# Two macaron layers with a three-group token mixer: first transposes of the FFN one product later, and copies, table switch and gate product of the mixer reordered

## The chip, the cores and the metric

The kernel runs on one core of a Trainium2 chip. The metric is the time of one execution on the device in microseconds (us). TensorE is called PE, its weight loads PEld, VectorE DVE, ScalarE ACT, GpSimd POOL and SyncE SP. DVE, ACT, POOL and SP each work through their own list of instructions in order.

## The reference

Two layers (L = 2) work on one sequence of 256 tokens of 1024 numbers, all in float32. Each layer is a half-step SwiGLU FFN, a token mixer and a second half-step FFN, each followed by a residual and a layer norm:

```
for l in range(2):
    x = layer_norm(a*x + 0.5*swiglu(x, wg[l,0], wu[l,0], wd[l,0]), ...)
    x = layer_norm(a*x + token_mix(x, ...), ...)
    x = layer_norm(a*x + 0.5*swiglu(x, wg[l,1], wu[l,1], wd[l,1]), ...)
swiglu(x) = (silu(x @ wg) * (x @ wu)) @ wd        # 1024 -> 2816 -> 1024
```

`token_mix` projects the stream once into the columns of three groups. Group A is a sparse attention with three branches: over compressed tokens (blocks of 32 tokens through a small GELU network), over selected blocks and over a window, merged by sigmoid gates. Group B subtracts the token from trailing means over 2, 4, 8 and 16 positions and multiplies by small matrices. Group C is a gated linear attention in chunks of 64 tokens: its output is normalised per head (root mean square over 64), and multiplied by a weight and by `silu(r)`. The three outputs side by side go through one output projection.

## The kernel before, in words

**Precision.** A float32 weight tile is cut into a high part (`wh`, a copy by ACT that rounds) and a low part (`wl`, what DVE has left after subtracting the high part). Every product is three matmuls of one pass each: high by high, high by low, low by high. These cuts (splits) of the weights are most of what ACT and DVE do. There are four buffers each for `wh` and `wl` (2 x 1024 columns) and four for the raw weights (`raw`); SP issues the loads in order, as buffers come free.

**The FFN.** The 2816 columns are 11 chunks of 256 gate and 256 up columns; the 256 tokens are two tiles t = 0, 1 of 128. Chunks 0 and 1 are computed first, plainly (`glu`), into the accumulator banks `acc` of each tile. The middle of the FFN is written out by hand in `PLAN`, and there PE's order is pinned to the program's. `S2`, `S4`, `S6` and `S8` open a block of two chunks c and c+1 by two tiles, done by a fast scheme with seven products instead of eight. A product is 12 matmuls of 512 columns and is named by a digit. The weights of some products are sums of weight blocks, which DVE forms in a tile `fa` (`b["s"]`):

- product 1 uses chunk c, first half (`fd`); product 5 the sum of `fd` and `fb` (L147), after which POOL has the DMA add a further block into `fb` for product 7;
- product 6 (`f6`) adds `fc` to the sum and splits it by `split_both` in two halves: two copies on ACT (L241) and two subtractions on DVE (L242);
- product 3 splits `fc` and product 7 `fb`, both in one wide subtraction (L234); product 2 loads two `raw` tiles and splits them (L172, L173);
- product 4 (`f4`) adds those two `raw` tiles to the sum (L180) and splits it again by `split_both`.

Other letters of `PLAN`: `a10` and `b10` are the first and second half of chunk 10 for both tiles (plain products; weight splits at L261 and L263); `T0`, `T2`, ... transpose the gated products of two chunks (`h_T`, L541) and split them into `hi` and `lo`; `d0`, `d1`, ... multiply them by the down weights (`down`), into two `acc` banks for each tile that ACT has seeded with the residual (L304). The list of weight units is filled from the same `PLAN`, so loads and splits follow its order.

PSUM has eight banks: for each tile one `g`, one `tr` and two `acc`. In the middle, `g` and `tr` form a list of free banks (`self.free`), from which blocks, T and a10 take theirs.

Gate products are made by `gate` (ACT L446, DVE L447 into `hh`) for plain chunks and by `gated` (L529, L530) for the blocks.

**The mixer.** Its order is the list `ORDER`, but here nothing is pinned on PE: a planner orders each engine's instructions by program order, by its own assumed durations, and by marks: `high_priority` lets an instruction go ahead of others that are ready, `issue_after(x)` (in the kernel also `after(x)`) places it behind x on the same engine. The steps that matter here:

- `chunk_gates`: PE transposes `c3`, DVE copies the result to `gaT` (L650), PE multiplies it by a small weight (L652).
- `compress`: a chain of small DVE operations on 30 numbers per partition computes the GELU: reciprocal, product (L722), then a copy that repeats the result four times into `grep` (L723), which PE uses as weights (L726).
- `attention`: for tile 1, eight items; each has scores on PE, an exponential on ACT (L853), a normalisation on DVE (L857), transposes on PE into the tile's one `tr` bank (L331) and a copy of them by ACT into `pT` (L900).
- the entry `s` of `ORDER` loads ACT's table with Silu (L1085), behind the last exponential (`m.last_exp`).
- `gla_out`: PE computes `ob`, ACT squares it (L954), DVE sums (L956, L957), POOL takes the power -1/2 (L958), DVE multiplies `ob` by it (L959) and then by `grs`, which holds weight and gate (L961), and PE transposes the product (L331).

Of the kernel before, what the change touches and what calls it, by code (L numbers as in the profile page):

```python
# [10 lines left out]
def _warn_once_fixed(msg, *args, **kwargs):  # L11
# [7 lines left out]
F32 = mybir.dt.float32  # L19
# [3 lines left out]
AF = mybir.ActivationFunctionType  # L23
# [14 lines left out]

PLAN = ("S2 1 T0 5 a10 6 3 b10 7 2 d0 4 S4 1 T2 5 d1 6 3 d2 7 2 4 S6 d3 1 T4 5 6 d4 3 7 2 4 "
        "S8 d5 1 T6 5 6 d6 3 T10 7 2 4 d7 T8").split()

LAST = (10, 8, 9)
# [12 lines left out]
def build(ctx, tc, d):  # L57
# [76 lines left out]
    def seven(l, f, c):  # L134


        b = {}

        def load(to, c, q, pool, name, tag):
            b[to] = pool.tile([128, 2048], F32, name=name, tag=tag, bufs=1)  # L140
            for h, a in enumerate(gate_up(l, f, c, q)):
                last_dma[0] = nc.sync.dma_start(out=b[to][:, h * 1024:(h + 1) * 1024], in_=a)

        def add(x, y=None):
            for h in range(2):
                s = slice(h * 1024, (h + 1) * 1024)
                DVE.tensor_add(out=b["s"][:, s], in0=(b["s"] if y is None else y)[:, s], in1=x[:, s])  # L147

        def f1():
            load("11", c, 0, act, "fd", "lnp")  # L150
            return split_wide(b["11"])

        def f5():
            load("12", c + 1, 0, cst, "fb", "s_w1")
            b["s"] = cst.tile([128, 2048], F32, name="fa", tag="ks")
            add(b["12"], b["11"])
            for h, a in enumerate(gate_up(l, f, c + 1, 1)):
                nc.gpsimd.dma_start(out=b["12"][:, h * 1024:(h + 1) * 1024], in_=a, accum_op=ALU.add)  # L158
            return split_both(b["s"])

        def f6():
            load("22", c + 1, 1, mix, "fc", "pT")
            add(b["22"])
            return split_both(b["s"])

        def f2():
            b["21"] = []
            u = split_tiles()
            for a, (wh, wl) in zip(gate_up(l, f, c, 1), u):
                raw = wp.tile([128, 1024], F32, name="raw", bufs=4)  # L170
                last_dma[0] = nc.sync.dma_start(out=raw, in_=a)
                ACT.activation(out=wh, in_=raw, func=AF.Copy)  # L172
                DVE.tensor_sub(out=wl, in0=raw, in1=wh.bitcast(F32))  # L173
                b["21"].append(raw)
            return u

        def f4():
            for h, raw in enumerate(b["21"]):
                s = slice(h * 1024, (h + 1) * 1024)
                DVE.tensor_add(out=b["s"][:, s], in0=b["s"][:, s], in1=raw)  # L180
            return split_both(b["s"])

        return {"1": f1, "5": f5, "6": f6, "7": lambda: split_wide(b["12"]), "3": lambda: split_wide(b["22"]),
                "4": f4, "2": f2}

# [48 lines left out]
        DVE.tensor_sub(out=wl, in0=raw, in1=wh.bitcast(F32))  # L234
        return in_halves(u)

    def split_both(raw):
        u = split_tiles()
        for h, (wh, wl) in enumerate(u):
            s = slice(h * 1024, (h + 1) * 1024)  # L240
            ACT.activation(out=wh, in_=raw[:, s], func=AF.Copy)  # L241
            DVE.tensor_sub(out=wl, in0=raw[:, s], in1=wh.bitcast(F32))  # L242
        return u

    def after(ins):
        return tc.issue_after(ins.ins) if ins else ExitStack()
# [41 lines left out]
    def pe(ins):  # L288

        if pinned[0]:  # L290
            tc.keep_in_program_order(ins)
        last_pe[0] = ins
# [114 lines left out]
    class Ffn:  # L407
# [126 lines left out]
        def h_T(self, t, g):  # L534
            src = self.hh.pop((t, g))
            if 2 * g == NCH - 1:
                src = src[:1]
            n = 2 * len(src)
            which, p = self.bank()
            for i, x in enumerate(x[:, j * 128:(j + 1) * 128] for x in src for j in range(2)):  # L540
                pe(PE.transpose(p[:, i * 128:(i + 1) * 128], x, ident))  # L541
            with tc.high_priority():
                hi = mix.tile([128, 4, 128], F32R, name="hi", tag="P", bufs=4)
                lo = mix.tile([128, 4, 128], F32R, name="lo", tag="b2", bufs=4)
                split(hi[:, 0:n], lo[:, 0:n], p[:, 0:128 * n].rearrange("p (a b) -> p a b", a=n))
            self.h[t, g] = (hi, lo)
            self.free.append(which)

        def down(self, t, c):
            accs = self.accs[t]  # L550
# [77 lines left out]
    def chunk_gates(m, t):  # L628
# [18 lines left out]

        p = transposes(t, [c3])
        gaT = mt(t, "gaT", [128, 128])
        DVE.tensor_copy(out=gaT, in_=p[:, 0:128])  # L650
        zp = bank("tr", t)
        PE.matmul(zp[:, 0:128], sm["wa2"], gaT, start=True, stop=True)  # L652
        az = mt(t, "az", [128, 128])
# [48 lines left out]
    def compress(m):  # L702
# [16 lines left out]
        ACT.activation(out=gs, in_=gs, func=AF.Exp, scale=-2.0 * GELU_C)  # L719
        DVE.tensor_scalar(out=gs, in0=gs, scalar1=1.0, scalar2=None, op0=ALU.add)  # L720
        DVE.reciprocal(out=gs, in_=gs)
        DVE.tensor_mul(out=gs, in0=gs, in1=xg)  # L722
        DVE.tensor_copy(out=grep[:, :, :, 0:15], in_=gs[:, None, :, :].to_broadcast([128, 4, 2, 15]))  # L723
        kp = bank("tr", 1)
        gflat = grep.rearrange("p a b c -> p (a b c)")
        PE.matmul(kp[:, 0:128], sm["w2k"], gflat, start=True, stop=True)  # L726
# [94 lines left out]
    def attention(m, t):  # L821

        v = m.t[t]
# [68 lines left out]
        def transpose_p(i):  # L892
            pj = P.pop(i).rearrange("p a b -> p (a b)")
            p = transposes(t, [pj[:, k * 128:(k + 1) * 128] for k in range(4)])
            j, gs = items[i]
            if j == 0:

                pool, tag = (wp, "fb") if t == 0 or gs[0] else (mix, "pT")
                PT[gs[0]] = pool.tile([128, 4, 4, 128], F32, name=f"pT{t}", tag=tag, bufs=1)
            ACT.activation(out=PT[gs[0]][:, :, j, :], in_=p.rearrange("p (a b) -> p a b", a=4), func=AF.Copy)  # L900

        def values():

# [33 lines left out]
    def gla_out(m, t):  # L937
# [18 lines left out]
        DVE.tensor_reduce(out=ms[:, 0:4], in_=sq, axis=AX.X, op=ALU.add)  # L956
        DVE.tensor_scalar(out=ms[:, 0:4], in0=ms[:, 0:4], scalar1=1.0 / 64, scalar2=RMS_EPS, op0=ALU.mult, op1=ALU.add)  # L957
        POOL.tensor_tensor(out=ms[:, 4:8], in0=ms[:, 0:4], in1=mhalf, op=ALU.pow)  # L958
        DVE.tensor_tensor(out=sq, in0=ob4, in1=ms[:, 4:8, None].to_broadcast([128, 4, 64]), op=ALU.mult)  # L959
        sqf = sq.rearrange("p a b -> p (a b)")  # L960
        DVE.tensor_mul(out=sqf, in0=sqf, in1=v["grs"])  # L961
        p = transposes(t, [sqf[:, 0:128], sqf[:, 128:256]])
        split(cth[:, 6:8, :], ctl[:, 6:8, :], p[:, 0:256].rearrange("p (a b) -> p a b", a=2))

# [109 lines left out]
    for l in range(L):  # L1074
        ffn(l, 0, sums, None)
        m = m0[0] if l == 0 else Mix(l)
        att = [attention(m, t) for t in range(2)]
        out = [wout(m, t) for t in range(2)]
        for op in ORDER.split():
            t = int(op[1]) if len(op) > 1 else 0  # L1080
            if op == "c":
                compress(m)
            elif op == "s":
                with tc.issue_after(m.last_exp.ins):
                    ACT.preload_act_table_set("silu_and_others")  # L1085
            elif op[0] == "a":
                run(att[t], 1)
            elif op[0] == "w":
                run(out[t], 1)
            else:  # L1090
                {"g": chunk_gates, "k": chunk_keys, "q": chunk_queries, "v": chunk_values, "r": chunk_rest, "p": pooling,
                 "l": gla_out}[op[0]](m, t)
        for g in att + out:
            assert next(g, "end") == "end"
        nxt = {}
        ffn(l, 2, m.sums, nxt)
        sums = nxt
# [85 lines left out]
```

## Time and profile before

| | |
|---|---|
| median of 3 runs | 951.4 us (949.92 to 951.83) |
| the profiled execution: time, span | 953.06 us, 951.3 us |
| mean granted clock of PE | 0.999 |
| instructions | 12752 |
| data read from HBM | 193.68 MB, 205 GB/s over the span |
| busy time of POOL | 57.4 us |

The profile shows one execution. The span runs from the first to the last instruction; the execution's own time has about 1.8 us more around it. A row of the timeline is: start in us from the span's start, duration in us, engine, line of the kernel, operation, output tile <- input tiles, shapes, how many in a row (x), and in brackets how long the engine sat idle before it and what ended that. A row of a group has the summed busy time, the mean in ns of one, and the idle time before them. In the rows of the waits stand the waiting engine, tile and line, then the releaser, then us in total, number and the longest.

### The profile page before, as it was taken

The numbers are of one execution on the slowest core, as the hardware profiler recorded it, in microseconds if no ns is written. First come the engines' busy times: TensorE is split into PE (matmuls) and PEld (weight loads), VectorE is DVE, ScalarE is ACT, GpSimd is POOL, SyncE is SP. The second block draws the span as 40 slices with busy tenths as digits, with TensorE's granted clock in tenths as the row PEclk, the third lists the DMA queues.
The fourth block names the chain that finished last, engine by engine and source line by source line (L and its number), as shares of the span: only waits on it lengthen the run. The fifth ranks groups of instructions, "written<-read, shape, count | busy, mean of one in ns | idle before, by whom it ended". The sixth has DMA issues, their size and how long they took to land.

```text
span 951.3 us, 12752 instructions
## 1 busy us (share of the span) xinstructions
PE 934.7 (98%) x4579; PEld 764.2 (80%) x4579; DVE 844.1 (89%) x1194; ACT 634.1 (67%) x993; POOL 57.4 (6%) x84
## 2 busy tenths in 40 slices
PE   9998999999999999999999999999999999999996
PEld 6887888888778888888887888888778788888885
DVE  5998999787978999999789999987889689999994
ACT  6866768475675767768467767764677467676770
POOL 0000010010101000010000000101000010000100
PEclk9999999999999999999999999999999999999999
DMA  9867786564435767776676786675634276867741
GB/s 327 270 223 231 234 258 236 194 225 159 142 122 172 199 229 226 240 231 237 216 214 208 235 242 244 177 251 177 229 105 131 91 224 198 246 231 220 232 151 45
DMA packets 56479, 195.57 MB, mean 206 GB/s; under 512 B 7136, under 2 KB 8160, under 8 KB 56160
## 3 DMA queue, kind: packets, MB, share of 16 engines
q1 hardware_dynamic: 49536, 170.11, 51.9%
q0 software_dynamic: 6736, 24.58, 12.1%
q8 instruction: 36, 0.59, 0.3%
q14 instruction: 27, 0.22, 0.1%
q10 hardware_dynamic: 144, 0.07, 0.0%
HBM read 193.68 MB, written 1.05 MB: 205 GB/s over the span
## 4 chain that ended last, share of the span: by engine, by line
PE 73%; DVE 13%; ACT 5%; DMA 4%; issue 3%; POOL 0%; DVEq 0%; SPq 0%; ACTq 0%
PE tr L461 15%; PE g L461 13%; PE acc L297 10%; PE acc L295 10%; PE acc L296 10%; DVE wl L263 3%; DMA fd<-in_wgu 3%; ACT wh L261 2%; DVE wl L234 2%; PE tr L331 2%; PE g L296 2%; DVE fa L147 2%; PE g L295 2%; PE g L297 1%; PE acc L322 1%
## 5 line engine op out<-in xcount | busy, mean ns | idle before, releaser
L261 ACT ACTIVATE wh<-raw 128x1024 fp32r<-128x1024 f32 (+2 forms) x194 | 195.7, 1034 | 77.7 <-PE acc L297 53.8
L263 DVE TENSOR_TENSOR wl<-raw,wh 128x1024 fp32r<-128x1024 f32 (+2 forms) x194 | 226.8, 1187 | 19.0 <-ACT wh L261 18.5
L241 ACT ACTIVATE wh<-fa 128x1024 fp32r<-128x1024 f32 x96 | 99.6, 1056 | 73.1 <-DVE fa L147 48.2
L295 PE MATMUL acc<-wh,hi 128*128 128x512 f32 x352 | 137.7, 391 | 0.0
L296 PE MATMUL acc<-wl,hi 128*128 128x512 f32 x352 | 137.3, 390 | 0.0
L297 PE MATMUL acc<-wh,lo 128*128 128x512 f32 x352 | 137.1, 389 | 0.0
L242 DVE TENSOR_TENSOR wl<-fa,wh 128x1024 fp32r<-128x1024 f32 x96 | 115.8, 1219 | 6.0 <-ACT wh L241 5.6
L297 PEld LDWEIGHTS acc<-wh,lo 128*128 128x128 f32 x352 | 66.1, 188 | 13.7
L296 PEld LDWEIGHTS acc<-wl,hi 128*128 128x128 f32 x352 | 66.1, 188 | 13.6
L295 PEld LDWEIGHTS acc<-wh,hi 128*128 128x128 f32 x352 | 66.1, 188 | 13.5
L295 PE MATMUL acc<-wh,xh 128*128 128x512 f32 x192 | 76.6, 399 | 0.3 <-ACT xh L308 0.3
L296 PE MATMUL acc<-wl,xh 128*128 128x512 f32 x192 | 76.1, 396 | 0.2 <-DVE wl L263 0.2
L297 PE MATMUL acc<-wh,xl 128*128 128x512 f32 x192 | 76.1, 397 | 0.0
L158 POOL DMA_DIRECT2D fb<-in_wgu x32 | 28.0, 874 | 459.4 <-DVE fa L147 270.3
L147 DVE TENSOR_TENSOR fa<-fd,fb 128x1024 f32<-128x1024 f32 x32 | 38.6, 1218 | 7.1 <-DMA fd<-in_wgu 7.0
L461 PE MATMUL tr<-wh,sb 128*128 128x512 f32 x128 | 42.5, 393 | 0.0
L297 PEld LDWEIGHTS acc<-wh,xl 128*128 128x128 f32 x192 | 36.2, 189 | 7.4 <-DVE xl L309 0.4
L461 PE MATMUL g<-wh,sa 128*128 128x512 f32 x128 | 42.1, 395 | 0.0
L461 PE MATMUL tr<-wh,sa 128*128 128x512 f32 x128 | 42.1, 395 | 0.0
L295 PEld LDWEIGHTS acc<-wh,xh 128*128 128x128 f32 x192 | 36.2, 189 | 7.3 <-ACT xh L308 0.5
L296 PEld LDWEIGHTS acc<-wl,xh 128*128 128x128 f32 x192 | 36.3, 189 | 7.1 <-DVE wl L263 0.5
L233 ACT ACTIVATE wh<-fb 128x1024 fp32r<-128x1024 f32 x32 | 32.4, 1058 | 13.9 <-PE tr L297 7.0
(288 smaller groups left out, 2166.7 us busy)
## 6 DMA issues: line engine op xcount, KB each, us to landing
raw<-in_wd SPq DMA_DIRECT2D x88, 512.0 KB, 4.7
raw<-in_wgu SPq DMA_DIRECT2D x79, 512.0 KB, 4.8
fd<-in_wgu SPq DMA_DIRECT2D x32, 512.0 KB, 6.3
fb<-in_wgu SPq DMA_DIRECT2D x32, 512.0 KB, 5.1
fc<-in_wgu SPq DMA_DIRECT2D x32, 512.0 KB, 4.3
fb<-in_wgu POOLq DMA_DIRECT2D x32, 512.0 KB, 6.7
raw<-in_win SPq DMA_DIRECT2D x32, 512.0 KB, 4.2
raw<-in_wout SPq DMA_DIRECT2D x16, 512.0 KB, 4.2
```

Source lines behind the costliest of these rows:

```text
L147: DVE.tensor_add(out=b["s"][:, s], in0=(b["s"] if y is None else y)[:, s], in1=x[:, s])
L158: nc.gpsimd.dma_start(out=b["12"][:, h * 1024:(h + 1) * 1024], in_=a, accum_op=ALU.add)
L233: ACT.activation(out=wh[:, s], in_=raw[:, s], func=AF.Copy)
L234: DVE.tensor_sub(out=wl, in0=raw, in1=wh.bitcast(F32))
L241: ACT.activation(out=wh, in_=raw[:, s], func=AF.Copy)
L242: DVE.tensor_sub(out=wl, in0=raw[:, s], in1=wh.bitcast(F32))
L261: ACT.activation(out=wh[:, s], in_=raw[:, s], func=AF.Copy)
L263: DVE.tensor_sub(out=wl[:, s], in0=raw[:, s], in1=wh[:, s].bitcast(F32))
L295: pe(PE.matmul(ps, xh, wh, start=start, stop=False, skip_group_check=seeded))
L296: pe(PE.matmul(ps, xh, wl, start=False, stop=False, skip_group_check=seeded))
L297: pe(PE.matmul(ps, xl, wh, start=False, stop=stop, skip_group_check=seeded))
L461: pe(PE.matmul(ps, a[:, k, :], w[:, s], start=first and k == 0 and n == 0, stop=k == 3 and n == 2, skip_group_check=True))
```

## The change

Four edits are in the FFN. `PLAN`'s first block becomes `S2 1 a10 5 T0 6 ...` instead of `S2 1 T0 5 a10 6 ...`; the weight units move with it. `h_T` takes for g = 0 (T0) an `acc` bank of the tile, the one left by chunks 0 and 1, instead of one of the free list. The transposes are written as matmuls with the transpose flag, of which only the first starts the bank. And the adds of `f4` are issued behind the last subtraction of `f6`.

Four are in the mixer: the copy `gaT` gets high priority; the last two operations of the GELU chain become one; the table load goes behind the last copy to `pT` (`m.last_pT`) instead of the last exponential; and in `gla_out` the product with `grs` comes first, from `ob`, and the product with the power second.

```
-PLAN = ("S2 1 T0 5 a10 6 3 b10 7 2 d0 4 S4 1 T2 5 d1 6 3 d2 7 2 4 S6 d3 1 T4 5 6 d4 3 7 2 4 "
+PLAN = ("S2 1 a10 5 T0 6 3 b10 7 2 d0 4 S4 1 T2 5 d1 6 3 d2 7 2 4 S6 d3 1 T4 5 6 d4 3 7 2 4 "
...
-            return split_both(b["s"])                      # f6
+            return split_both(b["s"], b)
...
-                DVE.tensor_add(out=b["s"][:, s], in0=b["s"][:, s], in1=raw)       # f4
+                with after(b["lo"]):
+                    DVE.tensor_add(out=b["s"][:, s], in0=b["s"][:, s], in1=raw)
...
-    def split_both(raw):
+    def split_both(raw, b=None):
...
-            DVE.tensor_sub(out=wl, in0=raw[:, s], in1=wh.bitcast(F32))
+            lo = DVE.tensor_sub(out=wl, in0=raw[:, s], in1=wh.bitcast(F32))
+            if b is not None:
+                b["lo"] = lo
...
-            which, p = self.bank()                          # h_T
+            which, p = self.bank() if g else (None, bank("acc", t))
...
-                pe(PE.transpose(p[:, i * 128:(i + 1) * 128], x, ident))
+                pe(PE.matmul(p[:, i * 128:(i + 1) * 128], x, ident, start=i == 0, stop=i == 2 * len(src) - 1, is_transpose=True,
+                             skip_group_check=True))
...
-            self.free.append(which)
+            if which:
+                self.free.append(which)
...
-        DVE.tensor_copy(out=gaT, in_=p[:, 0:128])
+        with tc.high_priority():
+            DVE.tensor_copy(out=gaT, in_=p[:, 0:128])
...
-        DVE.tensor_mul(out=gs, in0=gs, in1=xg)
-        DVE.tensor_copy(out=grep[:, :, :, 0:15], in_=gs[:, None, :, :].to_broadcast([128, 4, 2, 15]))
+        DVE.tensor_tensor(out=grep[:, :, :, 0:15], in0=gs[:, None, :, :].to_broadcast([128, 4, 2, 15]),
+                          in1=xg[:, None, :, :].to_broadcast([128, 4, 2, 15]), op=ALU.mult)
...
-            ACT.activation(out=PT[gs[0]][:, :, j, :], in_=p.rearrange("p (a b) -> p a b", a=4), func=AF.Copy)
+            m.last_pT = ACT.activation(out=PT[gs[0]][:, :, j, :], in_=p.rearrange("p (a b) -> p a b", a=4), func=AF.Copy)
...
-        DVE.tensor_tensor(out=sq, in0=ob4, in1=ms[:, 4:8, None].to_broadcast([128, 4, 64]), op=ALU.mult)
         sqf = sq.rearrange("p a b -> p (a b)")
-        DVE.tensor_mul(out=sqf, in0=sqf, in1=v["grs"])
+        DVE.tensor_mul(out=sqf, in0=ob[:, 0:256], in1=v["grs"])
+        DVE.tensor_tensor(out=sq, in0=sq, in1=ms[:, 4:8, None].to_broadcast([128, 4, 64]), op=ALU.mult)
...
-                with tc.issue_after(m.last_exp.ins):
+                with tc.issue_after(m.last_pT.ins):
                     ACT.preload_act_table_set("silu_and_others")
```

## The prediction, made before the changed kernel was run

> **What bounds the kernel now.** I read the engines' busy shares first, then the waits of TensorE (PE), then the timeline around each wait, on the engine that ends it.
>
> ```profile
> PE 934.7 (98%) x4579; PEld 764.2 (80%) x4579; DVE 844.1 (89%) x1194; ACT 634.1 (67%) x993; POOL 57.4 (6%) x84
> L461 PE MATMUL tr<-wh,sa 128*128 128x512 f32 x128 | 42.1, 395 | 0.0
> 93.54 8.16 PE tr L461 x36
> ```
>
> The last row is from the chain of waits: 36 matmuls in 8.16 us, one every 0.227 us, though one lasts 0.39 us (395 ns in the group). Matmuls overlap, so a wait costs PE the idle time shown plus the lost overlap, 0.39 - 0.23 = 0.16 us. In its dense stretches PE cannot go faster, and nearly all of the span is such stretches: time can only come from the places where PE waits. The waits of PE list them (engine, tile and line, then the releaser: us in total, times, longest):
>
> ```profile
> PE tr L461 <- DVE wl L242: 2.2, 1, 2.2
> PE tr L541 <- DVE hh L447: 1.6, 2, 1.1
> ...
> PE tr L331 <- ACT pT L900: 1.1, 2, 0.6
> PE tr L652 <- DVE gaT L650: 0.9, 2, 0.5
> PE tr L331 <- DVE sq L961: 0.6, 2, 0.3
> PE tr L461 <- DVE wl L234: 0.5, 1, 0.5
> ```
>
> These six are 6.9 us in 10 waits; with 0.16 us each they are worth 8.5 us. Every part of the change but the compression product points at one of them.
>
> **Part 1: the first transposes (T0) one product later, and chunk 10's first half (a10) before product 5.** T0 transposes the gated products of chunks 0 and 1. The last of these, hh of token tile 1, comes late because VectorE (DVE) takes its work in order. PE and DVE in the third FFN:
>
> ```profile
> 503.25 0.82 PE L541 MATMUL tr<-ident,hh 128*128 128x128 f32 x6
> 505.20 0.44 PE L541 MATMUL tr<-ident,hh 128*128 128x128 f32 x2 [1.14 <-DVE hh L447]
> 502.47 2.35 DVE L263 TENSOR_TENSOR wl<-raw,wh 128x1024 fp32r<-128x1024 f32 x2
> 504.74 0.41 DVE L447 SCALAR_TENSOR_TENSOR hh<-sg,acc 128x256 f32<-128x256 f32 x1
> 505.18 0.60 ACT L304 ACTIVATE acc<-x 128x512 f32<-128x512 f32 x1 [1.31 <-DVE hh L447]
> ```
>
> PE is through with product 1 at 503.25 and needs hh, which stands behind two weight splits until 505.1. In the new order a10 (24 matmuls, 24 x 0.227 = 5.4 us) and product 5 (12, 2.7 us) come in between: T0 comes 8.2 us later, 6 us after hh is there. What PE meets at 503.25 instead is a10, and the row at 502.47 is a10's own split: its first half is done at 503.7 and its second at 504.8, so even if DVE kept today's order PE would be held by some 0.2 us; with the units in the new order a10's split stands ahead of product 5's sums, and nothing is left. Two such waits stand in the list: 1.6 + 2 x 0.16 = 1.9 us. A third shows only as a wait of the weight load:
>
> ```profile
> PEld tr L541 <- DVE hh L447: 2.3, 3, 1.4
> ```
>
> With it T0 is worth 1.9 to 2.3 us; I take 2.1. The transposes themselves (as a matmul with the transpose flag, with one start for the bank instead of four) move the same columns and I cost them at nothing. The bank: T0 takes an accumulator bank that chunk 0 or 1 has left long before. The four seeds (L304, 0.60 us each on ScalarE, ACT) then take the next two banks of each tile, so one of two stands behind T0's evacuation, 8 us later than now. What waits for the seeds is d0, which follows products 6, 3, b10, 7 and 2: 4 x 2.7 + 5.4 = 16 us of PE. Evacuation and seeds (about 2.5 us each by these rows) fit into that, so cost nothing; past 16 us each us would be a PE wait in four FFNs. Today's seeds hold up ACT until hh is there (1.31 us in the row), which goes away but bounds nothing. Product 5's own sums, and the accumulating transfers on POOL that follow them, may come later by up to the 8.2 us by which their use is later; their user, product 7, is not moved.
>
> **Part 2: f4's adds not before f6's last subtraction (lo).** This is the largest wait, in the first FFN. PE, then DVE, then ACT:
>
> ```profile
> 83.11 0.50 PE L461 MATMUL tr<-wl,sa 128*128 128x512 f32 x1 [2.24 <-DVE wl L242]
> 85.31 0.50 PE L461 MATMUL tr<-wl,sb 128*128 128x512 f32 x1 [0.55 <-DVE wl L234]
> 76.15 1.23 DVE L242 TENSOR_TENSOR wl<-fa,wh 128x1024 fp32r<-128x1024 f32 x1
> 80.70 1.22 DVE L180 TENSOR_TENSOR fa<-fa,raw 128x1024 f32<-128x1024 f32 x1 [3.33 <-DMA raw<-in_wgu]
> 81.84 1.22 DVE L242 TENSOR_TENSOR wl<-fa,wh 128x1024 fp32r<-128x1024 f32 x1
> 82.98 2.28 DVE L234 TENSOR_TENSOR wl<-fc,wh 128x2048 fp32r<-128x2048 f32 x1
> 77.92 1.04 ACT L233 ACTIVATE wh<-fc 128x1024 fp32r<-128x1024 f32 x1
> ```
>
> The add at 80.70 stands in DVE's queue ahead of product 6's second subtraction (81.84) and waits 3.33 us for a weight load; PE waits for that subtraction. With the edge the subtraction runs near 78, ahead of PE's need at 80.7, and the 2.24 + 0.16 = 2.4 us go. What is late next is product 3's split of fc (82.98, 2.28 long). If it too passes the add (its input is ready at 77.92 + 1.04 = 78.96), the second wait (0.55 + 0.16 = 0.7) goes as well: 3.1 us. If the add is next after the subtraction and still waits until 80.70, the split starts at 81.84 instead of 82.98: PE gets 1.1 us in all. The same place in the second FFN has this order:
>
> ```profile
> 367.88 1.21 DVE L180 TENSOR_TENSOR fa<-fa,raw 128x1024 f32<-128x1024 f32 x1
> 369.02 2.28 DVE L234 TENSOR_TENSOR wl<-fc,wh 128x2048 fp32r<-128x2048 f32 x1
> ```
>
> There the add is ahead of the split, so I take 1.1, with 3.1 as the other end; below zero only by the third rival.
>
> **Part 3: gaT's copy at high priority.**
>
> ```profile
> 202.09 2.34 DVE L263 TENSOR_TENSOR wl<-raw,wh 128x1024 fp32r<-128x1024 f32 x2
> 205.10 0.29 DVE L650 COPY gaT<-tr 128x128 f32<-128x128 f32 x1
> ```
>
> The 0.29 us copy stands behind two splits (2.34) and two small operations. One place earlier than the second split it ends before PE wants it: 0.9 + 2 x 0.16 = 1.2 us over both layers. If the planner finds it ready no earlier, 0. I take 1.2.
>
> **Part 4: the table switch after the last pT copy instead of the last exponential.** ACT, then DVE and PE of the last transposes:
>
> ```profile
> 272.28 1.28 ACT L1085 ACT_TABLE_LOAD   x1
> 273.58 0.60 ACT L900 ACTIVATE pT<-tr 128x512 f32<-128x512 f32 x1
> 277.37 0.38 ACT L954 ACTIVATE sq<-tr 128x256 f32<-128x256 f32 x1 [0.24 <-PE tr L944]
> 283.00 0.60 ACT L308 ACTIVATE ch<-acc 128x512 fp32r<-128x512 f32 x1 [4.75 <-PE acc L322]
> 274.74 0.68 DVE L857 TENSOR_TENSOR P<-P,cf 128x512 f32<-128x512 f32 x1
> 275.89 0.60 PE L331 MATMUL tr<-ident,P 128*128 128x128 f32 x4
> ```
>
> The load holds the pT copy that frees PE's transposing bank: 1.1 + 2 x 0.16 = 1.4 us in both layers. Late next: the last transposes (275.89) would come 0.7 earlier, at 275.2, but their P ends at 275.42, so some 0.2 each may come back; I take 1.1. The load moves ahead of the square at 277.37 and delays it by about 1 us; the cover is the 4.75 us in which ACT is idle before 283.00, and the chain behind the square:
>
> ```profile
> 280.04 0.42 DVE L961 TENSOR_TENSOR sq<-sq,grs 128x256 f32<-128x256 f32 x1
> 282.80 0.38 PE L331 MATMUL tr<-ident,sq 128*128 128x128 f32 x2
> ```
>
> The product is done at 280.46 and PE wants it at 282.80: 2.3 us of cover, of which 1 is used.
>
> The row at 273.58 starts as the load ends. The Trainium skill ("ScalarE: Activation LUTs", section "What ACT_TABLE_LOAD costs") states 1.28 us for the load and as much again, 1.38 us, of drain. No such second part shows behind the load here. By the page the square would come 1.4 us later still and the cover would be used up; by an estimate from that figure each layer could then lose some 0.1 us of this part's gain, and the sum would be 0.2 smaller.
>
> **Part 5: gla_out's two products exchanged.** The product with grs goes before POOL's power instead of behind it.
>
> ```profile
> 294.62 1.02 POOL L958 TENSOR_TENSOR ms<-ms,mhalf 128x4 f32<-128x4 f32 x1 [5.00 <-DVE ms L957]
> 295.66 0.42 DVE L959 TENSOR_TENSOR sq<-tr,ms 128x256 f32<-128x256 f32 x1 [1.13 <-POOL ms L958]
> ```
>
> DVE is idle for 1.13 us while POOL works, and the 0.42 us product fits in there. The chain gets 0.45 us shorter, which is the whole wait: 0.6 + 2 x 0.16 = 0.9 us in both layers. Tile 0 has the cover of 2.3 us above and gains nothing.
>
> **Part 6: one operation for two in the compression.**
>
> ```profile
> 221.20 0.19 DVE L722 TENSOR_TENSOR tg<-tg,xg 128x30 f32<-128x30 f32 x1
> 221.43 0.22 DVE L723 COPY grep<-tg 128x120 f32<-128x120 f32 x1
> ```
>
> The chain loses one of two steps of some 0.2 us; PE's weight matmuls wait for it briefly. 0 to 0.2 us in each layer; I take 0.1, 0.2 in all.
>
> **Sum.** 2.1 + 1.1 + 1.2 + 1.1 + 0.9 + 0.2 = 6.6 us. The profiled execution took 953.06 us (its span 951.3), so 946.5; it lies 1.66 us above the median of the three runs (951.4), against which the forecast is 944.8. With all upper ends (2.3, 3.1, 1.2, 1.4, 0.9, 0.4) it is 9.3 us, 942.1. The unknown is what the planner, which orders DVE and ACT anew around every edit, does elsewhere: it is bounded by the waits of this profile, 0.3 to 2.4 us each.
>
> **Rivals.** (1) Only the pinned part works. PLAN's order on PE is written out and must change; the mixer's edits are wishes to the planner, whose costs may put the copy and the load where they cost as much. Then parts 1 and 2 are left, 3.2 us: 948.2. Against it: the table load has an explicit edge and part 5 changes the data flow itself.
>
> (2) The waits only move, because DVE is the bound. DVE is busy for 844.1 us, and a PE that comes earlier would meet splits that are not yet done. Then only DVE's own shorter work counts, 2 x 0.2 us: 951.0, no change. For it: five of the six waits above end on DVE or on what stands in its queue. Against it: each of them is an operation standing in the wrong place, with 107 us of DVE idle time over the span, and behind each wait the splits' buffers are freed by PE. The Trainium skill ("Perfetto Trace Analysis", section "Identifying the Most-Contended Engine") rates PE by its weight loads instead of its matmuls, here 80%, under DVE's 89%, and would make DVE the engine to relieve; the spacing of 0.227 us in the chain speaks against that.
>
> (3) Slower: f4's adds come later, and they free two of the four raw buffers into which SP loads the next weights, in order.
>
> ```profile
> SPq L256 <- DVE fa L180: 11.9, 7, 2.2
> L180 DVE TENSOR_TENSOR fa<-fa,raw 128x1024 f32<-128x1024 f32 x32 | 38.7, 1216 | 3.3 <-DMA raw<-in_wgu 3.3
> ```
>
> SP's queue already waits seven times for an add. There are 16 blocks (32 adds). If the adds slide behind another split and the loads reach PE late by one add, 1.2 us, in each block, that is 19 us less the 6.6: 964. It outweighs the gains from 0.41 us in each block on, and shows as slower from 0.53 on. Against it: in the second FFN the add already follows both subtractions, with no PE wait.
>
> **Chances.** Forecast (gain of 4.5 to 9.3 us) 0.55; rival 1 (2 to 4.5) 0.20; rival 2 0.15; rival 3 or other new waits 0.10. A change of under 0.2%, 1.9 us, cannot be told from none here. So faster 0.75, same 0.15, slower 0.10. The likeliest case alone spans 942 to 947; the range that leaves out no more than 2 in 10 goes on through rival 1 to where rival 2 begins: 941.8 to 950.2.
>
> **What would show it.** In the new profile's waits of PE the rows for hh, gaT, pT and sq L961 are gone; T0's transposes come 8 us after product 1 with no idle before them; around 78 us the second L242 of product 6 precedes the add, and what is left before product 3 is under 1.3 us; the table load stands behind the eighth pT copy; POOL's power has a DVE product beside it. I am wrong if PE's busy time falls by less than its waits, if new PE waits on wl or on a weight load stand in the middles of the FFNs, or if T0 waits for its bank.

## The result, and the profile of the changed kernel

The changed kernel took 946.0 us (median of five executions, 944.61 to 946.61) beside 951.62 us for the kernel before on the same chip (six, 949.92 to 952.24): a ratio of 0.9941, 95% interval 0.9927 to 0.9954, so 5.6 us less (4.4 to 6.9). Two later comparisons gave 0.9936 (0.9920 to 0.9952) and 0.9932 (0.9909 to 0.9954). Five executions of the whole study ran at a much lower granted clock (0.56 to 0.85) and are left out everywhere. The profiled execution took 945.39 us, its span 943.6.

The busy shares of the changed kernel, and the waits of PE (engine, tile and line, releaser: us in total, times, longest):

```profile
PE 933.4 (99%) x4579; PEld 764.4 (81%) x4579; DVE 843.6 (89%) x1192; ACT 633.3 (67%) x993; POOL 57.4 (6%) x84
```

```profile
PE acc L106 <- DVE zw L109: 1.2, 1, 1.2
PE tr L658 <- DVE gaT L656: 0.6, 2, 0.3
PE acc L298 <- ACT xh L311: 0.3, 1, 0.3
PE acc L299 <- DVE wl L266: 0.2, 1, 0.2
PE tr L732 <- PE acc L299: 0.2, 1, 0.2
PE acc L300 <- DVE lo L312: 0.2, 1, 0.2
```

Of the six waits that the prediction listed, those for hh, for wl (twice), for pT and for sq are gone from the list; gaT's has become smaller. DVE is as busy as before (844.1 then, 843.6 now), and the time fell all the same. Below, a "delay" of PE is the distance from the start of one matmul to the start of the next, less the usual one: 0.23 us behind a matmul of 512 columns, 0.11 us behind a transpose of 128. The two profiled spans are 951.3 us before and 943.6 after.

One of the signs by which the prediction would have called itself wrong was badly put: PE's busy time did fall by less (934.7 to 933.4, 1.3 us) than its listed waits (8.9 to 2.7, 6.2 us). A wait that goes takes idle time away, and that shows in the span, not in the busy time.

The middle of the first FFN, where the largest wait stood (timeline of the changed kernel, DVE, then one row of its chain: start, us, what):

```profile
75.50 1.23 DVE L243 TENSOR_TENSOR wl<-fa,wh 128x1024 fp32r<-128x1024 f32 x1
77.40 1.23 DVE L243 TENSOR_TENSOR wl<-fa,wh 128x1024 fp32r<-128x1024 f32 x1 [0.67 <-ACT wh L242]
78.54 2.29 DVE L235 TENSOR_TENSOR wl<-fc,wh 128x2048 fp32r<-128x2048 f32 x1
```

```profile
78.86 5.44 PE tr L464 x24
```

Both subtractions of product 6 and the split of `fc` for product 3 now run with no add between them, and PE goes through products 6 and 3 (24 matmuls in 5.44 us, 0.227 each) without a stop. In the third FFN T0 finds its input ready; DVE, then PE:

```profile
498.66 0.42 DVE L450 SCALAR_TENSOR_TENSOR hh<-sg,acc 128x256 f32<-128x256 f32 x1
506.41 1.03 PE L544 MATMUL acc<-ident,hh 128*128 128x128 f32 x8
```

hh is done 7.3 us before T0, and the eight transposes run in one go. The table load stands behind the eighth pT copy:

```profile
272.73 0.60 ACT L906 ACTIVATE pT<-tr 128x512 f32<-128x512 f32 x1 [1.68 <-PE tr L334]
273.35 1.28 ACT L1091 ACT_TABLE_LOAD   x1
274.64 0.38 ACT L960 ACTIVATE sq<-tr 128x256 f32<-128x256 f32 x1
```

Three places in the mixer did not do what was forecast: gaT, the compression product and the gla_out product. For each, the producer on DVE, PE's matmul ahead of the consumer and the consumer:

```profile
199.94 1.22 DVE L266 TENSOR_TENSOR wl<-raw,wh 128x1024 fp32r<-128x1024 f32 x1
200.84 0.39 PE L299 MATMUL acc<-wl,xh 128*128 128x512 f32 x1
201.19 0.29 DVE L656 COPY gaT<-tr 128x128 f32<-128x128 f32 x1
201.54 0.49 PE L658 MATMUL tr<-gaT,s_wa 128*128 128x128 f32 x2 [0.30 <-DVE gaT L656]
...
217.41 0.40 PE L299 MATMUL acc<-wl,xh 128*128 128x512 f32 x1
217.47 0.28 DVE L728 TENSOR_TENSOR grep<-tg,xg 128x120 f32<-128x120 f32 x1
218.01 0.46 PE L732 MATMUL tr<-grep,s_w2k 128*128 128x128 f32 x2 [0.20 <-PE acc L299]
...
290.11 1.02 POOL L964 TENSOR_TENSOR ms<-ms,mhalf 128x4 f32<-128x4 f32 x1 [5.00 <-DVE ms L963]
289.94 0.42 DVE L966 TENSOR_TENSOR sq<-tr,grs 128x256 f32<-128x256 f32 x1
291.17 0.43 DVE L967 TENSOR_TENSOR sq<-sq,ms 128x256 f32<-128x256 f32 x1 [0.81 <-POOL ms L964]
291.20 0.48 PE L298 MATMUL acc<-wh,ch 128*128 128x512 f32 x1
291.74 0.41 PE L334 MATMUL tr<-ident,sq 128*128 128x128 f32 x2
```

The copy of gaT still stands behind both splits; its delay is 201.54 - 200.84 - 0.23 = 0.47 us (0.62 before). The compression waits 0.37 us (0.31 before), though its chain lost an operation. The gla_out product with grs does run beside POOL's power, but a delay of 0.31 us is left (0.45 before). In all three PE's consumer stands one matmul earlier in PE's order than before: behind L299 instead of L297 (which is L300 now) for gaT and the compression, behind L298 instead of L296 (L299 now) for sq. Counted from the start of the trace, the first layer's consumers have 924, 1055 and 1474 matmuls ahead of them now, and had 925, 1056 and 1475.

### The profile page after: what moved, and what is told of

The parts are those of the page before. It is cut to its first block, busy times and chain, and to the rows that moved or that the text cites. A ratio compares the mean times of both kernels' runs of the same rounds, so it can differ in the third digit from the quotient of the medians.

```text
span 943.6 us, 12766 instructions
## 1 busy us (share of the span) xinstructions
PE 933.4 (99%) x4579; PEld 764.4 (81%) x4579; DVE 843.6 (89%) x1192; ACT 633.3 (67%) x993; POOL 57.4 (6%) x84
## 4 chain that ended last, share of the span: by engine, by line
PE 95%; ACT 2%; DVE 1%; DMA 1%; issue 0%; SPq 0%; DVEq 0%; ACTq 0%
PE g L464 16%; PE tr L464 15%; PE acc L300 14%; PE acc L298 14%; PE acc L299 14%; PE tr L334 3%; PE g L299 2%; PE g L298 2%; PE g L300 2%; PE acc L325 2%; PE tr L300 2%; PE tr L299 2%; PE tr L298 2%; PE tr L325 1%; PE g L544 1%; DMA raw<-in_wd 1%
## 5 line engine op out<-in xcount | busy, mean ns | idle before, releaser
L298 PE MATMUL acc<-wh,hi 128*128 128x512 f32 x352 | 137.7, 391 | 0.0
L300 PE MATMUL acc<-wh,lo 128*128 128x512 f32 x352 | 137.3, 390 | 0.2 <-DVE lo L312 0.2
L299 PE MATMUL acc<-wl,hi 128*128 128x512 f32 x352 | 137.3, 390 | 0.0
L300 PEld LDWEIGHTS acc<-wh,lo 128*128 128x128 f32 x352 | 66.1, 188 | 14.6 <-DVE lo L312 0.8
L299 PEld LDWEIGHTS acc<-wl,hi 128*128 128x128 f32 x352 | 66.1, 188 | 13.5
L298 PEld LDWEIGHTS acc<-wh,hi 128*128 128x128 f32 x352 | 66.1, 188 | 13.5
L299 PE MATMUL acc<-wl,xh 128*128 128x512 f32 x192 | 76.5, 398 | 0.2 <-DVE wl L266 0.2
L300 PE MATMUL acc<-wh,xl 128*128 128x512 f32 x192 | 76.7, 399 | 0.0
L298 PE MATMUL acc<-wh,xh 128*128 128x512 f32 x192 | 76.3, 397 | 0.4 <-ACT xh L311 0.3
L298 PEld LDWEIGHTS acc<-wh,xh 128*128 128x128 f32 x192 | 36.3, 189 | 7.5 <-ACT xh L311 0.5
L299 PEld LDWEIGHTS acc<-wl,xh 128*128 128x128 f32 x192 | 36.2, 189 | 7.4 <-DVE wl L266 0.8
L300 PEld LDWEIGHTS acc<-wh,xl 128*128 128x128 f32 x192 | 36.3, 189 | 7.0 <-DVE xl L312 0.5
L464 PE MATMUL g<-wh,sb 128*128 128x512 f32 x128 | 41.3, 389 | 0.0
```

Source lines behind the costliest of these rows:

```text
L298: pe(PE.matmul(ps, xh, wh, start=start, stop=False, skip_group_check=seeded))
L299: pe(PE.matmul(ps, xh, wl, start=False, stop=False, skip_group_check=seeded))
L300: pe(PE.matmul(ps, xl, wh, start=False, stop=stop, skip_group_check=seeded))
L464: pe(PE.matmul(ps, a[:, k, :], w[:, s], start=first and k == 0 and n == 0, stop=k == 3 and n == 2, skip_group_check=True))
```

## The experiments

My theory after this: a wait of PE that goes is a gain of its whole delay (against: DVE is the bound and waits only move); the gain of the FFN's two parts differs from execution to execution, because loads are involved (against: fixed by the order of instructions); and what is left in the mixer is set by where the planner puts PE's consumer, not by the producer (against: DVE's queue in front of the producer).

### One part at a time

**T0 alone.** The kernel before with PLAN, the accumulator bank and the flagged transposes:

```
-PLAN = ("S2 1 T0 5 a10 6 3 ...
+PLAN = ("S2 1 a10 5 T0 6 3 ...
...
-            which, p = self.bank()
+            which, p = self.bank() if g else (None, bank("acc", t))
```

> The kernel before with the FFN's first part alone: the new PLAN, the accumulator bank for T0 and the transposes as flagged matmuls; f4's adds and the mixer stay as before. Theory (a PE wait that goes is a gain of its idle time plus 0.16 us): the waits for hh go, 2.1 us, about 949.5 against 951.6, and PE waits nowhere new by more than 0.3 us. The wait for product 6's subtraction in the first FFN stays, 2.4 us or more, since nothing here moves the add. Rival (the waits only move, DVE is the bound): within 0.5 us of before. Third view: the new order of units alone already moves the add behind the subtraction, and the first FFN's wait goes too: 4.5 to 5.2 us less.

Measured: ratio 0.9983 (0.9972 to 0.9995), 1.6 us less (0.5 to 2.7). The waits of PE in this kernel have no row for hh any more, and the add's wait stays:

```profile
PE tr L461 <- DVE wl L242: 2.0, 1, 2.0
PE acc L106 <- DVE zw L109: 1.2, 1, 1.2
PE tr L331 <- ACT pT L902: 1.1, 2, 0.6
PE tr L654 <- DVE gaT L652: 0.9, 2, 0.5
```

So the third view (the new order of units alone moves the add) falls. The rival that waits only move (a gain within 0.5 us) has the trace against it, where the hh rows are gone and no new one took their place; the measured interval ends just where the rival does.

**f4's edge alone.**

```
+                with after(b["lo"]):
+                    DVE.tensor_add(out=b["s"][:, s], in0=b["s"][:, s], in1=raw)
```

> The kernel before with f4's adds behind f6's last subtraction, nothing else. The prediction's value was 1.1 us, the two traces show 3.1 us gone at this place. Theory: the 2.40 and 0.71 us of the profiled execution are what the place costs in ordinary executions too: 3.1 us less, about 948.5. Rival: that execution was 1.7 us above the median because the weight load landed late there; then ordinary executions lose 0.5 to 1.5 us at this place and the edge is worth that. Second rival: the waits only move (0).

Measured: 0.9973 (0.9963 to 0.9984), 2.6 us less (1.5 to 3.5). Both waits for wl are gone from its trace. That is near the theory's 3.1 us and excludes the prediction's 1.1; of the rival's 0.5 to 1.5 us the interval leaves the upper end alone.

**The mixer's four edits alone** (two of them shown):

```
+        with tc.high_priority():
+            DVE.tensor_copy(out=gaT, in_=p[:, 0:128])
...
-                with tc.issue_after(m.last_exp.ins):
+                with tc.issue_after(m.last_pT.ins):
```

> The kernel before with the mixer's four edits alone, FFN as before. The prediction's terms sum to 3.4 us (1.2 + 1.1 + 0.9 + 0.2). Theory from the traces: 1.9 us (table load 1.44, gaT 0.3, gla_out 0.28, compression -0.13), about 949.7; the waits for gaT and sq are still there, near 0.47 and 0.31 us each. Rival (each edit is worth its whole wait, and the new waits come from the FFN's edits): 3.4 us, 948.2.

Measured: 0.9975 (0.9962 to 0.9988), 2.4 us less (1.1 to 3.6); the interval holds both 1.9 and 3.4. The trace decides: with the old FFN the delays are again 0.46 and 0.47 us for gaT, 0.31 and 0.31 for sq, 0.47 and 0.22 for the compression. So they do not come from the FFN's edits. The three parts together make 1.6 + 2.6 + 2.4 = 6.6 us; the whole change measured 5.6 to 6.5.

**The table load put back**, in the changed kernel:

```
-                with tc.issue_after(m.last_pT.ins):
+                with tc.issue_after(m.last_exp.ins):
```

> The changed kernel with the table load behind the last exponential again, as before. The prediction took 1.1 us for this part (1.4 less what the last transposes give back). Theory: the wait of 0.72 us for the pT copy is back in both layers and nothing is given back, 1.4 us in all. Rival: 0.9 to 1.1 us, since the last transposes wait for their P when they come earlier.

One execution took 946.75 us. The load is back at its old place, and PE's transposes wait for the copy behind it (ACT, then PE):

```profile
268.34 1.28 ACT L1091 ACT_TABLE_LOAD   x1
269.63 0.60 ACT L906 ACTIVATE pT<-tr 128x512 f32<-128x512 f32 x1
270.28 0.66 PE L334 MATMUL tr<-ident,P 128*128 128x128 f32 x4 [0.56 <-ACT pT L906]
```

The delay is 0.72 us in each layer, 1.4 in all, and the changed kernel's trace has none at these or the last transposes: the whole of it is gained. (The time of one execution is too coarse to show 1.4 us by itself; this rests on the traces.)

Here the planner left the consumer where it was: the transposes that waited have 1339 matmuls ahead of them in the traces of before, of the changed kernel and of this one. The last transposes have 1348 ahead of them with the load at its old place and 1351 with the new one, so they ask three matmuls later.

### Is the first profile typical?

**The kernel before, unaltered, profiled a second time.**

> The kernel before, unaltered, as a second profiled execution. Theory: the mixer's waits and those of the gated products in the later FFNs come out the same to 0.1 us, since they are fixed by the order of instructions; the waits of the first FFN for product 6's subtraction and product 3's split, 2.40 and 0.71 us in the first profile, come out elsewhere between 0.7 and 3 us together, since the add in front of them waits for a load. Rival: they are fixed too, 3.1 us, and the spread of 948 to 956 us between executions lies elsewhere.

It took 952.31 us (953.06 the first time). The mixer's waits are the same to 0.02 us (gaT 0.62, pT 0.72, sq 0.46). The wait for product 6's subtraction is 2.48 us (2.40 the first time, but 0.94 in the trace of the mixer's edits alone, where the FFN is the same code). What I had not expected: the hh wait of the third FFN, 1.30 us in the first profile, is 0.22 here. DVE in the kernel before, first and second profile:

```profile
490.37 1.23 DVE L147 TENSOR_TENSOR fa<-fd,fb 128x1024 f32<-128x1024 f32 x1 [2.95 <-DMA fd<-in_wgu]
```

```profile
489.54 1.22 DVE L147 TENSOR_TENSOR fa<-fd,fb 128x1024 f32<-128x1024 f32 x1 [1.90 <-DMA fd<-in_wgu]
503.90 0.42 DVE L447 SCALAR_TENSOR_TENSOR hh<-sg,acc 128x256 f32<-128x256 f32 x1
503.50 1.31 PE L541 MATMUL tr<-ident,hh 128*128 128x128 f32 x8
```

In one execution the sum for product 5 waits 2.95 us for a load, in the other 1.90; everything behind it in DVE's queue moves with it, and hh starts at 504.74 or at 503.90. (PE, too, is through with product 1 at 503.25 or 503.50, 0.25 us later in the second.) So the "theory" of that expectation was half wrong: the waits of the gated products are not fixed by the order, they depend on loads as well. Over the four traces with the old T0 the hh delays add up to 2.1, 1.4, 1.4 and 0.2 us, and over the four with the old f4 the waits behind the add (products 6 and 3) to 3.1, 2.9, 1.7 and 2.5 us.

In two of these four the place cost more than its waits. PE in the second profile of before:

```profile
83.18 0.79 PE L461 MATMUL tr<-wl,sa 128*128 128x512 f32 x1 [2.32 <-DVE wl L242]
84.63 0.63 PE L461 MATMUL tr<-wl,sa 128*128 128x512 f32 x1
85.05 0.63 PE L461 MATMUL tr<-wh,sa 128*128 128x512 f32 x1
85.48 0.63 PE L461 MATMUL tr<-wh,sb 128*128 128x512 f32 x1
```

Behind the wait the matmuls start 0.43 us apart and last 0.63, and the granted clock of PE is 0.50 from 83.1 to 86.5 us. In the trace of T0 alone it is 0.50 from 83.6 to 87.0. In the other twelve traces it is 1.00 from the first few microseconds to the last few, in the first profile of before too, with nearly the same wait (2.24 us). With this the stretch from 80 to 89 us lost 3.4 and 4.2 us in the two profiles of before, 4.3 with T0 alone and 1.9 with the mixer's edits alone. What decides whether the clock falls is not shown; none of the ten traces with f4's edge has the fall, or the long wait.

The spread differs too. The kernel before ran from 948.14 to 956.25 us over the study, the changed one, with fewer executions, from 944.61 to 946.94. Which edit narrows it is not shown: side by side on one chip the range was 6.5 us for the kernel before (29 executions), and 1.5 with T0 alone, 3.1 with f4's edge alone and 4.0 with the mixer's edits alone (12 each).

### Producer or consumer?

**The consumers placed by hand**, producers as in the changed kernel; `at_slot` issues the held-back steps behind a given group of three matmuls (the comments say which they are):

```
+            slot["k", 1, 5] = rest  # gaT's matmul and what follows, behind group 5 of the keys
...
+        slot["v", 0, 5] = rest      # the compression's two matmuls, behind group 5 of the values
...
+            slot["o", 1, 1] = rest  # gla_out's transposes, behind group 1 of the third block
```

> The changed kernel with three consumers on PE placed by hand one to four matmuls later, in tile 1 for the first and third: the matmul of gaT behind the fifth group of three of the keys' projection, the compression's matmul behind the fifth group of the values' projection, and gla_out's transposes behind the first group of the third block of the output projection. Producers on DVE and ACT keep their place. Theory (what is left of these waits is PE's order: the planner puts the consumer where its model has the producer done, and that is 0.2 to 0.5 us too early): the waits of 0.47 + 0.47, 0.31 + 0.31 and 0.37 + 0.22 us go, 2.1 us, near 944.0 against 946.2 of the changed kernel. Rival (DVE's queue in front of the copy is the cause, and later consumers push the waits on to the next users, the gate chain and the last quarter of the output projection): within 0.5 us of the changed kernel, with new waits behind.

Measured: 0.9923 (0.9903 to 0.9942), 7.3 us under the kernel before; not told apart from the changed kernel by time. In the trace the delays for gaT and sq are gone and the compression's is 0.17 and 0 us, but two new ones of 0.31 and 0.24 us stand at zA, the compression's first input:

```profile
211.31 0.41 DVE L718 TENSOR_TENSOR zA<-zr,s_pe 128x256 f32<-128x256 f32 x1
211.82 0.31 PE L327 MATMUL tr<-zA,s_w 128*64 128x30 f32 x4
```

The gate chain behind gaT started later, DVE took a split ahead of it, and zA came after both. So a part of the rival is right: a consumer moved later can make another late.

**The producer alone made earlier**: in tile 1 the second subtraction of the split goes behind gaT's copy.

```
+        if t == 1:
+            with after(cp):
+                held.pop()()
```

> The changed kernel with the producer of gaT alone moved earlier: the second subtraction of the split goes behind the copy in tile 1, nothing else, so the copy ends 0.8 us earlier. Theory (the planner puts the consumer where it believes the producer done): the matmul of gaT moves forward on PE by four matmuls and the wait stays, 0.3 to 0.5 us in each layer; the time is that of the changed kernel. Rival (the wait was the split in front of the copy): the wait of 0.47 us is gone in both layers.

One execution took 946.59 us. DVE and PE:

```profile
199.67 1.23 DVE L270 TENSOR_TENSOR wl<-raw,wh 128x1024 fp32r<-128x1024 f32 x1
200.80 0.40 PE L302 MATMUL acc<-wh,xh 128*128 128x512 f32 x1
201.26 0.29 DVE L660 COPY gaT<-tr 128x128 f32<-128x128 f32 x1
201.61 0.49 PE L665 MATMUL tr<-gaT,s_wa 128*128 128x128 f32 x2 [0.41 <-DVE gaT L660]
```

Only one split stands in front of the copy, and the delay is larger: 201.61 - 200.80 - 0.23 = 0.58 us, in the second layer too. PE was given the matmul four places earlier (920 matmuls ahead of it instead of 924), as the theory has it. (All of this execution lies some 0.9 us later than that of the changed kernel; the copy is early against PE's stream.)

**Both sides, and the consumers without the producers' edits.** The first has the earlier copy and the three places (gaT's behind group 4); the second is the kernel before with the FFN's edits and the table load, none of the mixer's other three edits, and later places (groups 5 and 6, and the second of the third block). The third is the changed kernel, unaltered.

```
+            if hold:
+                held.append(lambda: DVE.tensor_sub(out=wl[:, s], in0=raw[:, s], in1=wh[:, s].bitcast(F32)))
+                continue
...
+            slot["k", 1, 4] = rest      # first kernel
+            slot["k", 1, 5] = rest      # second kernel
```

> The changed kernel with both sides of the three mixer places arranged: in tile 1 the second subtraction of the split that stood ahead of gaT's copy goes behind the copy (the producer earlier), and PE's consumers are placed by hand (gaT's matmul behind the fourth group of three of the keys' projection, the compression's behind the fifth of the values' projection, gla_out's transposes behind the first group of the third block of the output projection). Theory: the waits for gaT, sq and grep go and none takes their place before the compression's first matmuls (zA): 1.9 to 2.1 us under the changed kernel, about 944.1. Rival (DVE's queue is full, whatever is moved ahead makes another late): less than 0.7 us.

> The kernel before with the FFN's edits and the table load, without the mixer's other three (gaT at normal priority, gla_out's products and the compression's two operations in the old order), but with the three consumers placed later on PE by hand: gaT's matmul behind the fifth group of three, the compression's behind the sixth, gla_out's transposes behind the second. Theory: all three waits go though no producer is faster, and the time is that of the kernel with both sides arranged to 0.6 us, 944 to 945. Rival (the producers have to be faster): the waits of before stay at 0.45 to 0.6 us each, or their users wait, 946 to 948.

> The changed kernel unaltered, for the comparisons on the same chip, and as a second profiled execution of it. Theory: the mixer's waits come out the same to 0.05 us (0.47, 0.31, 0.37 and 0.22 us), since nothing in them depends on when a weight load lands; the first FFN differs from one execution to the next, by 0.3 to 1.5 us in waits at 70 and 170 us, since there the splits wait for loads. About 946.2.

Measured on one chip: the changed kernel 945.42 us (944.65 to 946.25), both sides 944.20, consumers alone 944.62; the three ratios to before are 0.9936, 0.9927 (0.9906 to 0.9949) and 0.9925 (0.9907 to 0.9943), whose intervals overlap. The second profile of the changed kernel has the same delays to 0.01 us (0.47, 0.47, 0.31, 0.31, 0.38, 0.22). The kernel with the consumers alone has none of the three waits, though its producers are those of before. DVE and PE at gla_out and the compression there:

```profile
290.73 0.43 DVE L983 TENSOR_TENSOR sq<-sq,grs 128x256 f32<-128x256 f32 x1
291.77 0.38 PE L339 MATMUL tr<-ident,sq 128*128 128x128 f32 x2
...
217.27 0.22 DVE L741 COPY grep<-tg 128x120 f32<-128x120 f32 x1
218.12 0.38 PE L747 MATMUL tr<-grep,s_w2k 128*128 128x128 f32 x2
```

The old order of operations is done 0.6 us before PE asks. The rival that the producers have to be faster falls. Of the 2.2 us of delays that went, about half stayed as a gain by the traces' spans (942.9 us for the changed kernel, 941.8 with both sides, 941.5 with the consumers alone): zA took back 0.4 to 0.5 us, and most of the rest lies at the start and at the end of the first FFN, where loads are waited for.

**Two more places.** The first kernel, with the compression's start behind group 1 of the values' projection, and the last half split of the last down chunk behind hi and lo of T8. The edit does two things more: the compression's weight matmul moves from group 5 to group 6, and from `d7` on the program takes the weight units one further ahead (`ahead`):

```
+        units.append(lambda: [split_half(a, w, u, hold=late and h, later=t8[0] if last and h else (None, None))
+                              for h, (a, u) in enumerate(zip(src, split_tiles()))])
...
+                            if x == "d7":
+                                ahead[0] = 2
...
+            slot["v", 0, 6] = rest
+        slot["v", 0, 1] = first
```

> The kernel with both sides of the three mixer places arranged, plus two places that its trace still shows: the compression's matmuls on zA start behind the first group of three of the values' projection (they waited 0.22 and 0.21 us), and in each FFN the last half split of the last down chunk goes behind the hi and lo of the last transposes (T8), since in the first FFN that split waits for its load with hi and lo behind it (0.71 us of PE in that execution, 0.3 to 0.8 in five others). Theory: 0.4 us and 0.3 to 0.7 us less than the kernel without these two, about 943.3, and no PE wait at 169 us. Rival: the waits at zA only move to the compression's later matmuls, and the late load holds up PE at the split's own use instead: no change against 944.2.

> The changed kernel unaltered, beside the kernel with all places arranged on the same chip: about 945.4 to 946.2, so 2 us above it by the theory and 1 us by the rival.

Measured on one chip: 942.77 us (942.24 to 943.21) beside 945.95 for the changed kernel (945.42 to 946.94); ratios 0.9895 (0.9878 to 0.9913) and 0.9932 (0.9909 to 0.9954). That is 3.2 us less where 2 were expected, the fastest kernel of the study; its slowest execution lies 2.2 us under the changed kernel's fastest of this comparison. Its waits of PE:

```profile
PE acc L106 <- DVE zw L109: 1.2, 1, 1.2
PE acc L310 <- ACT xh L323: 0.6, 1, 0.6
PE acc L311 <- DVE wl L278: 0.2, 1, 0.2
```

Only waits at the start of the kernel are left in the list, and none at zA. Of the difference of the two traces' spans (944.1 and 941.0 us) 2.1 us are the delays of the three mixer places, and 0.7 us an idle stretch of PE at 8 us, at the start of the kernel, that only the changed kernel's execution had. What T8's place and the units taken further ahead bring is not settled: PE does not wait there now, but in this execution of the changed kernel it lost only 0.16 us there. DVE's busy time is 843.3 us, a share of 90%, and it still is not the bound.

## Why the prediction came out as it did

The time was right: 944.8 us forecast, 946.0 measured, inside the range and inside the likeliest case's own. That the sum came so near is partly luck: by the traces part 2 gave 2.0 us more than its term, and parts 3, 5 and 6 together 1.8 us less. By its own parts (us; delays in the first pair of traces, and the part alone against before):

| part | predicted | the two traces | measured alone |
|---|---|---|---|
| 1, T0 later | 2.1 | 2.1 | 1.6 (0.5 to 2.7) |
| 2, f4's adds | 1.1 | 3.1 | 2.6 (1.5 to 3.5) |
| 3, gaT | 1.2 | 0.3 | |
| 4, table load | 1.1 | 1.4 | |
| 5, gla_out | 0.9 | 0.3 | |
| 6, compression | 0.2 | -0.1 | |
| 3 to 6 | 3.4 | 1.9 | 2.4 (1.1 to 3.6) |
| sum | 6.6 | 7.1 | 6.6; the whole change 5.6 to 6.5 |

Part 1: the mechanism held at every step: a10 fits in, the bank is free, the seeds cost nothing (no PE wait at d0), and PE does not wait for product 5's late sums. But 2.1 us was the price in that one execution; it was 0.2 to 2.1 us in four.

Part 2: the mechanism was right and the value was wrong, 1.1 us for 3.1. "If the add is next after the subtraction" was taken over from the second FFN; in the first FFN the split of `fc` (78.54) passed the adds too. The upper end, 3.1 us, is what came. What the prediction leaves out is the clock: it prices the wait with the idle time and 0.16 us, but in two of four traces the stretch lost 4.2 and 4.3 us, with the granted clock at 0.50 behind the wait.

Parts 3, 5 and 6 failed in the same step: "one place earlier ... it ends before PE wants it" and "the chain gets 0.45 us shorter, which is the whole wait" treat the moment at which PE asks as fixed. In the mixer PE's order is not pinned, and at these places the planner moves the consumer forward with the producer: seen directly for gaT, where a copy 0.8 us earlier left 0.58 us, and from the other side where old producers with later consumers left none. What stays as a delay, 0.2 to 0.6 us at these places, I take for the error of the planner's assumed durations; these were not looked at, so that last step is argued, not shown. In part 3 the copy, moreover, passed only the small operations: it still stands behind both splits. The prediction named the planner as the unknown, but let it act "elsewhere".

Part 4: 1.1 for 1.4. The consumer kept its place in PE's order, so the whole delay was gained, and the last transposes were put three matmuls later, so the 0.2 us per layer that they were to give back did not come. The load stands 0.02 us behind the copy at 272.73 (0.60 long), and the row at 274.64 starts 0.01 us after the load of 1.28 us ends. The Trainium skill ("ScalarE: Activation LUTs", section "What ACT_TABLE_LOAD costs") adds 1.38 us of drain; no such part shows here, in front of the load or behind it, and the trace decides.

The rivals: that the waits only move falls with the first three experiments, each faster by itself (the first by 0.5 us at least), and with the last, where every listed wait but those of the start is gone while DVE stays at 843 us. The Trainium skill ("Perfetto Trace Analysis", section "Identifying the Most-Contended Engine") rates PE by its weight loads and by its share of the peak rate. By the weight loads, the measure that the prediction took, it would have named DVE, at 89% against 81%; the runs do not agree, as PE's delays went and the time with them. In a small form the rival is true: at zA 0.4 to 0.5 of 2.2 us came back until that place was arranged as well. The slower case, raw buffers held up by the adds, does not show: f4's edge alone makes the kernel faster. The premise under all parts, that PE's dense stretches cannot be shortened, was not tested; the first profile shows only that behind none of the matmuls of form `128*128 128x512 f32` the next one starts sooner than 0.224 us after it.

Against which time the sum was made mattered as well: the first profile of before was at 953.06 us, with the waits for hh and for the add at the most that any of the four traces has, so the two spans differ by 7.7 us where the medians differ by 5.6.

## What to carry to other kernels

Before a wait is priced, ask who fixed the moment at which the waiting engine asks: where the order was pinned, the whole wait was gained; where a planner orders both, it moved the consumer too at three places of four, and there the surer edit was to place the consumer a few matmuls later. A wait with an operation in front that itself waits for a load has a size for each execution: profile twice before it becomes a term of a sum. And look behind a long wait, at the spacing of the matmuls and the granted clock: the wait may cost more than its idle time.

## What the runs showed of the hardware that I had not expected

In two executions of the same program DVE waited 2.95 and 1.90 us for the same weight load and went on at 490.37 and 489.54 us after the start. The PE wait 13 us later was 1.30 and 0.22 us: DVE came 0.84 us earlier to it in the second, and PE 0.25 us later. The delays at gaT, pT and sq repeated to 0.02 us from one execution to the next.

A wait of PE of some 2 us can be followed by 3.4 us at half the granted clock (0.50, matmuls 0.43 us apart instead of 0.23): behind 2.32 us of idle time in one execution of the kernel before, and behind 2.02 and 0.42 us with T0 alone, but not behind 2.24 and 0.55 us in another execution of the kernel before.
